# The last two output blocks by token halves, and the places of pass 3 moved into pass 1

## The chip, the cores and the metric

The kernel runs on one NeuronCore of one Trainium2 chip. The metric is the device time of one execution in microseconds (us), lower is better. The engines are named as in the profile: PE (TensorE matmul), PEld (its weight loads), DVE (VectorE), ACT (ScalarE), POOL (GpSimd) and SP, whose queue issues most transfers.

## The reference, cut to what matters

One decoder layer on 512 tokens of 1024 features, float32: token mixing (block-sparse attention and gated DeltaNet, merged), an output projection, and a mixture of experts. What the change touches begins at the output projection:

```python
x = x + g1 * (m @ w_out)                       # 8 output blocks of 128 features
h = rms_norm(x, norm2_w) * (1.0 + sc2) + sh2
pg = softmax(h @ w_rg + b_rg)                  # 4 groups: the best one
le = (h @ w_re + b_re).reshape(T, 4, 8)        # 8 experts in it: the best two
...
a = silu(h @ w_e_gate[e]) * (h @ w_e_up[e])    # for each chosen expert e
y += w2 * (a @ w_e_down[e])
x = x + g2 * y
out = rms_norm(x, final_norm_w)
```

## The kernel before

The program is traced in Python by a framework that orders each engine's instructions itself: an instruction that is traced earlier has priority, and one whose inputs are modelled as late may be passed by later ones. Two helpers pin the order. `tc.issue_after(x)` queues what is traced in it behind `x`, on `x`'s engine only. `Prog.step` does so for the last PE and the last SP instruction so far, so that all steps form one chain on PE and one on SP.

**`project_out`.** The features of `m` lie in SBUF as high and low parts. Output block `i` (128 features, all 512 tokens) is 8 x 3 matmuls (`mm3`, lines 138 to 140) of 128x512 into a PSUM tile `pj`; then DVE adds it to the residual `x1`, ACT squares it, and DVE adds the squares up in `asq`. The logits of blocks 0 to 5 are made in pairs, after blocks 1, 3 and 5 (line 1078), and the blocks 0 to 3 are turned to rows by `rows(i)` (four transposes, line 1050, and a copy on ACT). Block 7 alone is made in two halves of 256 tokens (`half`): `logits(h)` adds the half, makes its logits (1113) and sums of squares (1044), the inverse norm (`rsqrt`, 152 to 156), and then `choose(h)` (1218 to 1231) finds group and experts on DVE. A few matmuls on the identity (`warm`, line 214) are fillers. After the second half blocks 4 to 7 are turned to rows, and the rows are written to DRAM (`xd`).

**`moe`, up to pass 0.** `spread` (8 transposes), `route` (a filler, then `count`: for each token, how many before it chose the same expert, 10 small matmuls, and `pos0`), `sort` (counts per expert), `first_match` (line 1733: eight compares that make a one-hot matrix `ohf` from the places, and the split of the norms in three parts `MR`), `sorted`, a filler. The row gathers of pass 0 are matmuls of the rows with `ohf` (`first_rows`, line 1753), four feature blocks at a time.

**The passes.** Each of the 13 passes takes 128 places, in two to four experts: `up` (eight steps `block(k)`, line 1796, gate and up products), `gate`, `features` of the next pass (transposes, 1718, and copies on ACT and DVE), `add` of the pass before (1870 to 1872), `turn`, `down` (1847). For a pass from 3 on, `match(p)` (1645) compares on DVE, `places(p)` (1670, 1673) and `weights(p)` (1702, 1704) are small matmuls and reductions, and `fetch(p)` (POOL) gathers rows from `xd`. The expert weights come in units of 1 MB through a ring of 18 slots (line 1005, SP queue); 18 units are loaded ahead, and a slot is loaded again when its last product is done. Inside `up(0)`, `first_steps(k)` does ahead of block `k`: gathers, `places(1)`, `places(2)` (k = 0), the expert order (k = 2), `places(0)` (4) and `weights(0)` (7). Behind pass 0 stand `weights(1)`, `weights(2)`, `match(3)`, `places(3)` and `fetch(3)`, and only then `up(1)`.

Of the kernel before, what the change touches and what calls it, by code (L numbers as in the profile page):

```python
# [93 lines left out]
class Prog:  # L94
# [912 lines left out]
    def project_out(self):  # L1007
# [3 lines left out]
        with tc.tile_pool(name="ps_out", bufs=1, space=PSUM, reuse_waits="tile") as pp:  # L1011
# [40 lines left out]
            for i in range(7):  # L1052
                wh, wl = self.unit_w(None, self.wo[i])
                ps = pp.tile([128, 512], F32, name="pj", bufs=2)
                for k in range(8):
                    self.mm3(ps, wh[:, k], wl[:, k], self.mhi[:, k], self.mlo[:, k], k == 0, k == 7)
# [18 lines left out]
                if i in (1, 3, 5):  # L1075

                    for g in range(2):
                        mm(tiles(lt[64 * g:64 * g + 64]), w6[:, i - 1 + g], blk(i - 1 + g), start=i == 1, stop=i == 5)
                    if i == 5:
                        nc.scalar.activation(lT, tiles(lt), AF.Copy)  # L1080
                elif i == 6:
                    pr[0] = pp.tile([128, 512], F32, name="rt0")[:, 0:36]
                    for t in range(4):
                        mm(pr[t], lT[:, t], sel, start=True, stop=False)
                        mm(pr[t], x1[:, t], self.wr[:, 6], start=False, stop=False)
                if i in (1, 3):
                    rows(i - 1)
                    rows(i)
                if i == 3:
                    nc.scalar.dma_start(xv[:, :, 0:512], self.acc[:, :, 0:512])  # L1090
                if i == 6:
                    psq = pp.tile([128, 512], F32, name="tr", bufs=2)
                    for t in range(4):
                        sums(psq[:, t:t + 1], asq, t)
                    v.tensor_scalar(ss, psq[:, 0:4], 1.0 / D, EPS, op0=OP.mult, op1=OP.add)

            wh, wl = self.unit_w(None, self.wo[7])
            half = [pp.tile([128, 512], F32, name="pj", bufs=2) for _ in range(2)]
            x1 = blk(7)

            def products(h, ks):
                c = slice(256 * h, 256 * h + 256)
                for k in ks:
                    self.mm3(half[h][:, 0:256], wh[:, k], wl[:, k], self.mhi[:, k, c], self.mlo[:, k, c], k == 0, k == 7)

            def logits(h):
# [5 lines left out]
                for t in ts:  # L1112
                    mm(pr[t], x1[:, t], self.wr[:, 7], start=False, stop=True)
# [631 lines left out]
    def first_rows(self, *ks):  # L1745
# [3 lines left out]
        for k in ks:  # L1749
            ps[k] = self.bank()  # L1750
# [185 lines left out]
```

## Time and profile before

| | us |
|---|---|
| median of 3 runs | 724.14 (722.12 to 724.37) |
| the profiled execution | 724.38 |
| its span, first to last instruction | 722.5 |
| PE busy | 692.8 (96%) |
| DVE busy | 485.5 (67%) |
| ACT busy | 283.0 (39%) |
| moved by DMA | 183.12 MB, mean 253 GB/s |

Matmuls overlap one another, and their ends are modelled: the start of one to the start of the next is what one costs, and a busy PE is not PE at its peak. The idle time in brackets behind a row is that of its engine just before it, with what ended it. The granted clock is the share of full speed that TensorE was given in a stretch.

### The profile page before, as it was taken

Reading aid. Unit: us, or ns where it says so; the run is one execution under the profiler, and the core shown is the slowest. Engines: PE = TensorE matmul, PEld = TensorE weight load, DVE = VectorE, ACT = ScalarE, POOL = GpSimd, SP = SyncE. Lnnn points to the kernel's source line nnn. Section 1 sums busy time; section 2 is a strip of 40 time slices with the busy share of each in tenths; the row PEclk is TensorE's granted clock in tenths of the full one; section 3 lists DMA queues with packets and bytes.
Section 4 is the critical chain, followed back from the end, with each engine's and each line's share of the span. In section 5 each row is a group of like instructions: output and inputs, shape, how many; then the busy total and the mean of one; then the engine's idle time right before and its main releaser. Section 6 shows DMA issues by size and latency. Waiting matters only on the chain. (4 is left out here: it accounts for less than half of the span.)

```text
span 722.5 us, 10988 instructions
## 1 busy us (share of the span) xinstructions
PE 692.8 (96%) x3939; PEld 481.7 (67%) x3939; DVE 485.5 (67%) x1243; ACT 283.0 (39%) x554; POOL 36.1 (5%) x43
## 2 busy tenths in 40 slices
PE   7999999999999899999999999998899999999995
PEld 5887868878798777876778867793444444554531
DVE  6987669968447677578766744284577766777654
ACT  5745357652233224367652323143122222322352
POOL 0002000520000000000000000100000000000000
PEclk9999999999999999999999999999999999999998
DMA  9942221058765772361168998068799999999994
GB/s 357 394 168 69 97 85 62 30 149 295 215 235 191 250 251 89 120 232 60 44 215 282 340 422 354 2 237 322 277 351 418 418 415 404 419 417 418 427 418 190
DMA packets 47756, 183.12 MB, mean 253 GB/s; under 512 B 11786, under 2 KB 12330, under 8 KB 34514
## 3 DMA queue, kind: packets, MB, share of 16 engines
q1 hardware_dynamic: 40930, 169.65, 62.3%
q10 hardware_dynamic: 4896, 8.51, 3.3%
q0 software_dynamic: 1872, 4.23, 1.6%
q8 instruction: 32, 0.52, 0.3%
q14 instruction: 26, 0.21, 0.1%
HBM read 175.63 MB, written 9.33 MB: 256 GB/s over the span
## 5 line engine op out<-in xcount | busy, mean ns | idle before, releaser
L138 PE MATMUL pj<-hR,uR 128*128 128x512 f32 x304 | 122.3, 402 | 1.5 <-DVE qk L762 1.5
L140 PE MATMUL pj<-hR,uS 128*128 128x512 f32 x304 | 122.1, 402 | 0.0
L139 PE MATMUL pj<-hR,uR 128*128 128x512 f32 x304 | 122.0, 401 | 0.0
L143 ACT ACTIVATE uR<-uF 128x1024 fp32r<-128x1024 f32 x48 | 50.8, 1060 | 104.1 <-PE pj L139 97.3
L1796 PE MATMUL gu<-ra,uS 128*64 128x512 f32 (+1 forms) x368 | 85.0, 604 | 1.4 <-DMA ra<-w_e 1.4
L144 DVE TENSOR_TENSOR uS<-uF,uR 128x1024 fp32r<-128x1024 f32 x48 | 58.4, 1219 | 25.8 <-ACT uR L143 24.1
L138 PEld LDWEIGHTS pj<-hR,uR 128*128 128x128 f32 x304 | 57.3, 188 | 14.2 <-issue 1.9
L140 PEld LDWEIGHTS pj<-hR,uS 128*128 128x128 f32 x304 | 57.3, 188 | 12.5 <-DVE uS L144 0.4
L139 PEld LDWEIGHTS pj<-hR,uR 128*128 128x128 f32 x304 | 57.3, 188 | 11.9 <-issue 0.3
L1872 DVE TENSOR_TENSOR accF<-accF,cb 128x512 f32<-128x512 f32 x96 | 59.7, 680 | 6.3 <-PE cb L1871 5.4
L219 DVE SCALAR_TENSOR_TENSOR sgF<-sgF,misc 128x1024 f32<-128x1024 f32 x32 | 38.9, 1218 | 12.7 <-DMA sgF<-w_mod 12.7
L1796 PEld LDWEIGHTS gu<-ra,uS 128*64 128x64 f32 (+1 forms) x368 | 25.0, 125 | 32.5 <-issue 27.8
L1823 DVE SCALAR_TENSOR_TENSOR uS<-uS,meta,gu 128x256 f32<-128x256 f32 x13 | 6.2, 480 | 55.1 <-ACT uS L1818 55.1
L1860 ACT ACTIVATE uR<-p2F 128x512 fp32r<-128x512 f32 x24 | 15.1, 632 | 67.2 <-DVE p2F L1858 63.3
L1870 PE MATMUL cb<-uR,oht 128*128 128x512 f32 x96 | 40.0, 416 | 0.0
L1871 PE MATMUL cb<-uR,oht 128*128 128x512 f32 x96 | 37.9, 395 | 0.0
L1796 PE MATMUL gu<-rb,uS 128*32 128x512 f32 (+1 forms) x136 | 32.5, 593 | 0.0
L1818 ACT ACTIVATE uS<-gu 128x256 f32<-128x256 f32 x13 | 5.0, 384 | 64.9 <-PE gu L1796 64.9
L138 PE MATMUL pj<-mR,uR 128*128 128x512 f32 (+1 forms) x72 | 27.3, 379 | 0.0
L409 DVE SCALAR_TENSOR_TENSOR dF<-dF,c_cols 128x512 f32<-128x512 f32 x36 | 26.6, 748 | 0.9
L139 PE MATMUL pj<-mR,uR 128*128 128x512 f32 (+1 forms) x72 | 27.0, 375 | 0.0
L140 PE MATMUL pj<-mR,uS 128*128 128x512 f32 (+1 forms) x72 | 26.8, 372 | 0.0
(437 smaller groups left out, 1346.0 us busy)
## 6 DMA issues: line engine op xcount, KB each, us to landing
ra<-w_e SPq DMA_DIRECT2D x54, 1024.0 KB, 10.6
rb<-w_e SPq DMA_DIRECT2D x25, 1024.0 KB, 10.7
uF<-w_in SPq DMA_DIRECT2D x38, 512.0 KB, 3.3
sgF<-w_mod SPq DMA_DIRECT2D x32, 512.0 KB, 4.8
rc<-w_e SPq DMA_DIRECT2D x15, 1024.0 KB, 8.1
sF<-w_mod SPq DMA_DIRECT2D x8, 1024.0 KB, 9.0
gd<-sgF ACTq DMA_DIRECT2D x16, 256.0 KB, 2.8
gF<-gd SPq DMA_DIRECT2D x8, 512.0 KB, 4.5
```

The costliest lines, as they stand in the source:

```text
L138: mm(ps, whi, xhi, start=first, stop=False)
L139: mm(ps, whi, xlo, start=False, stop=False)
L140: mm(ps, wlo, xhi, start=False, stop=last)
L143: self.nc.scalar.activation(hi, raw, AF.Copy)
L144: self.nc.vector.tensor_sub(lo, raw, hi.bitcast(F32))
L219: self.nc.vector.scalar_tensor_tensor(raw, raw, 1.0, self.cact, op0=OP.mult, op1=OP.mult, accum_out=self.mod[:, ot:ot + 1])
L409: nc.vector.scalar_tensor_tensor(a, r[:, k:k + 512], w[:, k:k + 1], a, op0=OP.mult, op1=OP.add)
L1796: nc.tensor.matmul(gu[r], xe[:, k, r], w[:, k % 4], start=k == 0, stop=k == 7)
L1860: i1 = nc.scalar.activation(self.yhi[:, c], self.yf[:, c], AF.Copy)
L1870: nc.tensor.matmul(pc, self.oht[:, ts], self.yhi[:, c], start=True, stop=False)
L1871: nc.tensor.matmul(pc, self.oht[:, ts], self.ylo[:, c], start=False, stop=True)
L1872: nc.vector.tensor_add(self.acc[:, t, c], self.acc[:, t, c], pc)
```

## The change

Blocks 6 and 7 are both made by halves of the tokens: first half of block 6, sums of what came before, first half of block 7, second half of block 6, `logits(0)`, second half of block 7, `logits(1)`. Each half has its own sums of squares over both blocks. The pairs of logits are put inside the products of the next block (ahead of k = 2, or k = 4 of block 6). `count`, `first_match` and the first four gathers of pass 0 are split into tokens 0 to 255 and 256 to 511, and the first half's are traced ahead of the second half's count. `weights(0)` and `scale(1)`, `features(1, 0)` move into `up(0)`; `weights(1)`, `weights(2)`, `match(3)`, `places(3)`, `fetch(3)` and `match(4)` into `up(1)`. The fillers keep their sizes.

```diff
                 for t in range(4):
...
                 nc.scalar.activation(blk(i), p, AF.Copy)
-            for i in range(7):
+            def pair(i):
+                w = next(x for x in reversed(nc.cur_bb.bb.instructions) if x.engine == mybir.EngineType.PE)
+                for g in range(2):
+                    with tc.issue_after(w):
+                        w = mm(tiles(lt[64 * g:64 * g + 64]), w6[:, i + g], blk(i + g), start=i == 0, stop=i == 4).ins
+                if i == 4:
+                    nc.scalar.activation(lT, tiles(lt), AF.Copy)
+                else:
+                    with tc.issue_after(w):
+                        rows(i)
+                        rows(i + 1)
+                    if i == 2:
+                        nc.scalar.dma_start(xv[:, :, 0:512], self.acc[:, :, 0:512])
+                return w
+            for i in range(6):
                 wh, wl = self.unit_w(None, self.wo[i])
...
                 for k in range(8):
-                    self.mm3(ps, wh[:, k], wl[:, k], self.mhi[:, k], self.mlo[:, k], k == 0, k == 7)
+                    with ExitStack() as es:
+                        if k == 2 and i in (2, 4):
+                            es.enter_context(tc.issue_after(pair(i - 2)))
+                        self.mm3(ps, wh[:, k], wl[:, k], self.mhi[:, k], self.mlo[:, k], k == 0, k == 7)
                 x1 = blk(i)
...
                 if i == 0:
...
                         self.load(12)
...
                     self.load(1)
-                if i in (1, 3, 5):
...
+            ws = [self.unit_w(None, self.wo[i]) for i in (6, 7)]
+            two = [pp.tile([128, 512], F32, name="pj", bufs=2) for _ in range(2)]
+            def products(j, h):
                 c = slice(256 * h, 256 * h + 256)
-                for k in ks:
-                    self.mm3(half[h][:, 0:256], wh[:, k], wl[:, k], self.mhi[:, k, c], self.mlo[:, k, c], k == 0, k == 7)
+                wh, wl = ws[j]
+                for k in range(8):
+                    with ExitStack() as es:
+                        if (k, j, h) == (4, 0, 0):
+                            es.enter_context(tc.issue_after(pair(4)))
+                        self.mm3(two[j][:, c], wh[:, k], wl[:, k], self.mhi[:, k, c], self.mlo[:, k, c], k == 0, k == 7)
+            def added(j, h):
+                x1 = blk(6 + j)[:, 2 * h:2 * h + 2]
+                v.scalar_tensor_tensor(x1, tiles(two[j])[:, 2 * h:2 * h + 2], self.mod[:, 22 + j:23 + j], x1,
+                                       op0=OP.mult, op1=OP.add)
+                nc.scalar.activation(sq[:, 2 * j:2 * j + 2], x1, AF.Square)
+            def sums_before():
+                pr[0] = pp.tile([128, 512], F32, name="rt0")[:, 0:36]
+                for t in range(4):
+                    mm(pr[t], lT[:, t], sel, start=True, stop=False)
+                psq = pp.tile([128, 512], F32, name="tr", bufs=2)
+                for t in range(4):
+                    sums(psq[:, t:t + 1], asq, t)
+                v.tensor_scalar(ss, psq[:, 0:4], 1.0 / D, EPS, op0=OP.mult, op1=OP.add)
             def logits(h):
                 c, ts = slice(2 * h, 2 * h + 2), (2 * h, 2 * h + 1)
-                v.scalar_tensor_tensor(x1[:, c], half[h][:, 0:256].rearrange("p (t s) -> p t s", t=2), self.mod[:, 23:24],
-                                       x1[:, c], op0=OP.mult, op1=OP.add)
-                nc.scalar.activation(sq[:, c], x1[:, c], AF.Square)
                 psq = pp.tile([128, 512], F32, name="tr", bufs=2)
+                for j in range(2):
+                    for t in ts:
+                        mm(pr[t], blk(6 + j)[:, t], self.wr[:, 6 + j], start=False, stop=j == 1)
                 for t in ts:
-                    mm(pr[t], x1[:, t], self.wr[:, 7], start=False, stop=True)
-                for t in ts:
-                    sums(psq[:, t:t + 1], sq, t)
+                    for j in range(2):
+                        mm(psq[:, t:t + 1], sq[:, 2 * j + t % 2], self.ones[:, 0:1], start=j == 0, stop=j == 1)
                 v.scalar_tensor_tensor(ss[:, c], psq[:, c], 1.0 / D, ss[:, c], op0=OP.mult, op1=OP.add)
...
                 return w
-            products(0, range(8))
-            products(1, range(SPL))
+            products(0, 0)
+            added(0, 0)
+            sums_before()
+            products(1, 0)
+            added(1, 0)
+            products(0, 1)
             logits(0)
-            products(1, range(SPL, 8))
+            added(0, 1)
+            products(1, 1)
+            added(1, 1)
             w = logits(1)
...
                 for i in range(4, 8):
...
         selb = self.selb
...
         self.step(self.warm, self.gu.tile([128, 512], F32, name="gu"), self.ident, W2)
-        self.step(self.count, self.pos0)
-    def count(self, pos):
+    def count(self, pos, ts=range(4)):
         nc, v, selb, sel = self.nc, self.nc.vector, self.selb, self.sel
...
         ps = self.tr.tile([128, 512], F32, name="tr")
-        for t in range(4):
+        for t in ts:
             r = ps[:, 32 * t:32 * t + 32]
...
             nc.tensor.matmul(r, self.sut, selb[:, t], start=t == 0, stop=True)
-        v.tensor_scalar(sel, selb, -4096.0, 4096.0, op0=OP.mult, op1=OP.add)
-        v.tensor_tensor(fl(pos), fl(sel), ps[:, 0:128], op=OP.add)
+        c = slice(ts[0], ts[-1] + 1)
+        v.tensor_scalar(sel[:, c], selb[:, c], -4096.0, 4096.0, op0=OP.mult, op1=OP.add)
+        v.tensor_tensor(fl(pos[:, c]), fl(sel[:, c]), ps[:, 32 * ts[0]:32 * ts[-1] + 32], op=OP.add)
     def sort(self):
...
         self.last, self.after_down, self.fin = {}, (), {}
...
         self.step(self.route)
+        self.ohf, self.oh0 = V(self.uS, 4, [4, 128]), self.scratch(4, 64).bitcast(BF16)
+        self.rows_of = {k: self.bank() for k in range(4)}
+        self.step(self.count, self.pos0, (0, 1))
+        self.first_match((0, 1))
+        self.step(self.gather_first, (0, 1), range(4))
+        self.step(self.count, self.pos0, (2, 3))
         self.step(self.sort)
-        self.first_match()
+        self.first_match((2, 3))
+        self.first_parts()
         self.sorted()
...
         for x in self.xg:
...
                     for x in self.after_down:
...
                     self.scale(p + 1)
-            if 0 < p < NP - 3:
+            if 1 < p < NP - 3:
                 self.match(p + 3)
...
                 self.step(self.finish_init)
...
                     for x in self.after_down:
...
                     self.step(self.alike, p)
-            self.up(p, between=self.first_steps if p == 0 else None)
...
+            self.up(p, between=self.first_steps if p == 0 else self.second_steps if p == 1 else None)
             self.gate(p)
             if p + 1 < NP:
-                self.step(self.features, p + 1, 0)
-                if p == 0:
-                    self.step(self.features, 1, 1)
+                self.step(self.features, p + 1, int(p == 0))
             else:
...
             if p:
...
                     self.step(self.finish_last, h)
...
             self.step(self.load, len(PASSES[p]) - (p == 0))
-            if p == 0:
...
         self.last = {}
         self.rest()
...
                 nc.vector.tensor_scalar(xe[:, k], pt[:, j], self.A2[:, k:k + 1], self.sh2[:, k:k + 1],
                                         op0=OP.mult, op1=OP.add)
-    def first_match(self):
-        self.ohf, self.oh0 = self.view(self.uS, 4, [4, 128]), self.scratch(4, 64).bitcast(BF16)
-        for t in range(4):
+    def first_match(self, ts):
+        for t in ts:
             for e in range(2):
...
                                                  op0=OP.is_equal, op1=OP.mult)
+        self.at_match = i.ins
+    def first_parts(self):
         r, v = self.T(4), self.nc.vector
-        with self.tc.issue_after(i.ins):
+        with self.tc.issue_after(self.at_match):
             v.tensor_copy(r, self.rs2)
...
                     v.tensor_tensor(r, r, self.MR[:, :, j], op=OP.subtract)
-        self.at_match = i.ins
     def first_rows(self, *ks):
-        nc = self.nc
-        ps = {}
+        nc, ps = self.nc, self.rows_of
         for k in ks:
-            ps[k] = self.bank()
...
+            if k not in ps:
+                ps[k] = self.bank()
+        self.gather_first((2, 3) if ks[0] == 0 else range(4), ks)
         for k in ks:
...
                                  scale=self.A2[:, k:k + 1])
+    def gather_first(self, ts, ks):
+        for t in ts:
+            for k in ks:
+                self.nc.tensor.matmul(self.rows_of[k][:, 0:128], self.acc[:, t, 128 * k:128 * k + 128], self.ohf[:, t],
+                                      start=t == 0, stop=t == 3)
     def first_steps(self, k):
...
         elif k == 4:
...
             self.step(self.places, 0)
-        elif k == 7:
             self.step(self.weights, 0)
+        elif k == 6:
+            with self.tc.issue_after(self.at_tables):
+                self.scale(1)
+            self.step(self.features, 1, 0)
+    def second_steps(self, k):
+        if k == 3:
+            for i in (1, 2):
+                self.step(self.weights, i)
+            self.match(3)
+        elif k == 5:
+            self.step(self.places, 3)
+            self.fetch(3)
+            self.match(4)
     def up(self, p, experts=None, part=None, between=None):
```

## Rows read from the trace of the kernel before

**Rows 1.** The page's part 2: share of the 16 DMA engines in tenths and the bytes per second, in 40 equal slices of 18.06 us.

```profile
DMA  9942221058765772361168998068799999999994
GB/s 357 394 168 69 97 85 62 30 149 295 215 235 191 250 251 89 120 232 60 44 215 282 340 422 354 2 237 322 277 351 418 418 415 404 419 417 418 427 418 190
```

**Rows 2.** The view of busy time by stretch: us of the stretch, its length, then the busy us of PE, PEld, DVE, ACT and POOL (instructions in brackets), the granted TensorE clock, the mean share of the DMA engines and GB/s. The stretches are the last output blocks, the routing up to the first expert product, the gap behind pass 0, the first products of pass 1, and most of the passes behind.

```profile
455.00:472.00 17.00, 17.00 (x108) 14.10 (x109) 5.53 (x13) 3.19 (x6) 0.95 (x1) 1.00 0.00 1
472.00:489.20 17.20, 16.26 (x170) 15.56 (x168) 15.26 (x93) 9.18 (x20) 1.22 (x1) 1.00 0.78 270
...
503.70:507.70 4.00, 0.78 (x26) 0.69 (x24) 3.81 (x11) 1.87 (x3) 0.00 (x0) 1.00 1.00 363
507.70:516.40 8.70, 8.70 (x37) 2.63 (x33) 1.78 (x8) 0.00 (x0) 0.99 (x1) 0.80 0.55 171
...
532.00:688.00 156.00, 155.29 (x1053) 74.46 (x1049) 107.80 (x241) 42.40 (x92) 7.91 (x8) 1.00 1.01 416
```

**Rows 3.** The timeline of the SP queue, which issues the expert weights' loads, each as soon as its slot is free (start, us, queue, line, count).

```profile
493.40 0.93 SPq L1005 DMA_DIRECT2D ra<-w_e  x2
...
503.82 0.33 SPq L1005 DMA_DIRECT2D ra<-w_e  x1
...
513.12 1.50 SPq L1005 DMA_DIRECT2D ra<-w_e  x2
```

**Rows 4.** The timeline at the end, PE's weight load of the last pass's last products, with what ended the idle time ahead of it in brackets.

```profile
708.56 0.27 PEld L1847 LDWEIGHTS cb<-ra,uS 128*32 128x32 f32 x5 [0.16 <-DMA ra<-w_e]
```

**Rows 5.** PE's timeline from the end of pass 0 to the first products' end of pass 1, and for comparison the first products of pass 3 from their start (542.72) to the next instruction behind them (549.73).

```profile
503.68 0.35 PE L1702 MATMUL tr<-p2F,uS 128*128 128x6 bf16 x8
507.25 0.35 PE L1670 MATMUL tr<-MC,uS 128*128 128x1 bf16 x8 [3.22 <-DVE uS L1645]
507.74 5.35 PE L1796 MATMUL gu<-ra,uS 128*64 128x512 f32 x16
...
516.46 0.65 PE L1718 MATMUL tr<-ct,uF 128*128 128x128 f32 x4
...
542.72 0.63 PE L1796 MATMUL gu<-rc,uS 128*32 128x512 f32 x3
...
549.73 0.66 PE L1718 MATMUL tr<-ct,uF 128*128 128x128 f32 x4
```

**Rows 6.** DVE's timeline in the gap behind pass 0.

```profile
505.92 0.51 DVE L1704 TENSOR_REDUCE meta<-tr 64x1 f32<-64x3 f32 x3
506.44 0.76 DVE L1645 TENSOR_TENSOR uS<-ct,p2F 128x384 bf16<-128x384 f32 x2
...
508.63 0.88 DVE L1645 TENSOR_TENSOR uS<-ct,p2F 128x128 bf16<-128x128 f32 x2
```

**Rows 7.** Busy time by stretches of 2 us behind the gap, columns as in rows 2.

```profile
506.00:508.00 2.00, 0.74 (x18) 0.66 (x20) 1.96 (x7) 0.00 (x0) 0.00 (x0) 1.00 0.90 295
508.00:510.00 2.00, 2.00 (x8) 0.52 (x6) 1.48 (x8) 0.00 (x0) 0.57 (x1) 0.54 0.34 139
510.00:512.00 2.00, 2.00 (x8) 0.61 (x6) 0.00 (x0) 0.00 (x0) 0.42 (x1) 0.61 0.49 113
```

**Rows 8.** ACT's timeline between the first products and the down products of pass 0, and PE's first down product.

```profile
498.26 1.51 ACT L1722 ACTIVATE uS<-tr,mod,A 128x128 f32<-128x128 f32 x4 [0.23 <-PE tr L1718]
499.65 0.40 ACT L1832 ACTIVATE uS<-gu 128x256 f32<-128x256 f32 x1
...
500.10 0.64 PE L1847 MATMUL cb<-uR,uS 128*64 128x512 f32 x1 [1.06 <-ACT uS L1832]
```

**Rows 9.** PE's timeline in the output blocks: two products of 512 columns (block 6), then two of 256 (block 7).

```profile
462.31 0.40 PE L139 MATMUL pj<-mR,uR 128*128 128x512 f32 x1
462.55 0.39 PE L140 MATMUL pj<-mR,uS 128*128 128x512 f32 x1
...
471.79 0.28 PE L139 MATMUL pj<-mR,uR 128*128 128x256 f32 x1
471.90 0.28 PE L140 MATMUL pj<-mR,uS 128*128 128x256 f32 x1
```

**Rows 10.** PE's timeline from the last output product to the first expert product: fillers (L214), sums, transposes (L1050, L1536), counts (L1249), row gathers (L1753), places (L1670).

```profile
472.02 1.05 PE L214 MATMUL pj<-ct 128*128 128x128 f32 x8
...
473.31 0.59 PE L1044 MATMUL tr<-ct,oF 128*128 128x1 f32 x4
...
477.00 1.50 PE L214 MATMUL gu<-ct 128*128 128x128 f32 x12
479.05 0.18 PE L1249 MATMUL tr<-selb,sut 128*128 128x32 bf16 x1 [0.55 <-ACT p2F L1537]
...
480.67 3.74 PE L1753 MATMUL cb<-uS,accF 128*128 128x128 f32 x32
484.24 0.34 PE L1670 MATMUL tr<-MC,uS 128*128 128x1 bf16 x8
...
489.22 0.65 PE L1796 MATMUL gu<-ra,uS 128*64 128x512 f32 x2
```

**Rows 11.** The same time on ACT (the two banks of `spread` are copied out) and DVE (the eight compares of `first_match`, and the last of the parts that `places` reads).

```profile
478.42 1.06 ACT L1537 ACTIVATE p2F<-tr 128x512 f32<-128x512 f32 x2
...
479.96 1.87 DVE L1733 TENSOR_SCALAR uS<-ct,p2F,rs 128x64 f32<-128x64 f32 x8
...
483.83 0.15 DVE L1740 CAST p2F<-p2F 128x4 bf16<-128x4 f32 x1
```

More of the change, by code (lines that the diff above doesn't have):

```diff
@@ L1074, in project_out @@
                     self.load(1)
-                if i in (1, 3, 5):
[L1077 to L1082, printed above, removed]
-                    for t in range(4):
-                        mm(pr[t], lT[:, t], sel, start=True, stop=False)
-                        mm(pr[t], x1[:, t], self.wr[:, 6], start=False, stop=False)
@@ L1086, in project_out @@
[L1086 to L1092, printed above, removed]
-                    for t in range(4):
-                        sums(psq[:, t:t + 1], asq, t)
-                    v.tensor_scalar(ss, psq[:, 0:4], 1.0 / D, EPS, op0=OP.mult, op1=OP.add)
-            wh, wl = self.unit_w(None, self.wo[7])
@@ L1244, in count @@
         ps = self.tr.tile([128, 512], F32, name="tr")
-        for t in range(4):
+        for t in ts:
             r = ps[:, 32 * t:32 * t + 32]
@@ L1404, in moe @@
                     self.step(self.alike, p)
-            self.up(p, between=self.first_steps if p == 0 else None)
-            if p == 0:
-                with tc.issue_after(self.at_tables):
-                    self.scale(1)
+            self.up(p, between=self.first_steps if p == 0 else self.second_steps if p == 1 else None)
             self.gate(p)
             if p + 1 < NP:
-                self.step(self.features, p + 1, 0)
-                if p == 0:
-                    self.step(self.features, 1, 1)
+                self.step(self.features, p + 1, int(p == 0))
             else:
@@ L1448, in moe @@
             self.step(self.load, len(PASSES[p]) - (p == 0))
-            if p == 0:
-                for i in (1, 2):
-                    self.step(self.weights, i)
-                self.match(3)
-                self.step(self.places, 3)
-                self.fetch(3)
         self.last = {}
@@ L1742, in first_match @@
                     v.tensor_tensor(r, r, self.MR[:, :, j], op=OP.subtract)
-        self.at_match = i.ins
     def first_rows(self, *ks):
-        nc = self.nc
-        ps = {}
+        nc, ps = self.nc, self.rows_of
         for k in ks:
-            ps[k] = self.bank()
-        for t in range(4):
-            for k in ks:
-                nc.tensor.matmul(ps[k][:, 0:128], self.acc[:, t, 128 * k:128 * k + 128], self.ohf[:, t],
-                                 start=t == 0, stop=t == 3)
+            if k not in ps:
+                ps[k] = self.bank()
+        self.gather_first((2, 3) if ks[0] == 0 else range(4), ks)
         for k in ks:
```

4 lines of the change are left out of this document (removed).

## Prediction

> **What bounds the kernel now.** I read the page's slices first. The DMA engines stand still around 455 to 472 us and then, from the first expert pass on, run at over 400 GB/s to the end [rows 1]. Next the busy time by stretch: from 532 to 688 us PE is busy 155.29 of 156.00 us and the DMA share is 1.01, so both are full and neither can be squeezed there [rows 2]. The reader is to see the two places where one of them is not: from 472.0 to 489.2 us the DMA share is 0.78, and from 507.7 to 516.4 us it is 0.55, which is 3.9 us of idle DMA.
>
> The idle comes from the SP queue. A weight load is issued when PE has freed its slot, at 493.40, at 503.82 and then only at 513.12 us [rows 3]. So ahead of 532 us PE sets when the loads go out, and behind it all that is left is a fixed amount of loads and products that slides with them. At the end the last weight loads of the last pass are still waited for, by 0.16 us, at 708.56 us [rows 4]: PE and the loads arrive together. A microsecond that PE wins ahead of 516 us is therefore a microsecond of the end, as long as there is idle DMA time to move the loads into. That makes the sum a sum of PE's time from 455 to 516 us.
>
> **The change, part 1: later places moved.** Pass 0 ends with PE's `weights` at 503.68 us. Then PE waits 3.22 us, for the compare of `match(3)` on DVE, before `places(3)` at 507.25 us and the first products of pass 1 at 507.74 us [rows 5]. That compare came last because DVE first had the reductions (to 506.43 us) and then took 0.76 us [rows 6]. The wait has a second cost: the granted clock was 1.00 up to 508 us, and after the wait 0.54 and 0.61 in the two stretches from 508 to 512 us [rows 7], so part of that time ran at the lower of the two levels, 1.2 GHz in place of 2.4. The first products of pass 1 took 516.46 - 507.74 = 8.72 us, those of pass 3 only 549.73 - 542.72 = 7.01 us [rows 5]: 1.71 us more.
>
> With the change `weights(1)` and `weights(2)` stand ahead of block 3 of pass 1's first products and `places(3)` ahead of block 5, so the first products can follow pass 0 at once; their input was written during pass 0. From 503.68 to 516.46 us is 12.78 us now. It becomes 7.01 us of products, 0.35 us for the two `weights` and 507.74 - 507.25 = 0.49 us for `places(3)` [rows 5], together 7.85 us. **The gain is 4.9 us.** What must hide: `match(3)` now has to run on DVE between block 3 and block 5. Two blocks are 2 x 7.01/8 = 1.75 us; the reductions and the compare took about 0.65 and 0.76 us, 1.41 us together [rows 6], so the margin is some 0.3 us less what signals cost. If that fails, PE stops inside pass 1 instead. `match(4)` (some 1.4 us of DVE) moves behind it and is needed only after the first products end. `fetch(3)` is issued on POOL with nothing queued behind it; its 0.5 MB takes 1.3 us at the 416 GB/s of the full stretch and falls into the stretch with 3.9 us idle [rows 2].
>
> `features(1, 0)` moves into pass 0's products ahead of block 6: four transposes, about 0.5 us more for PE there. In return ACT's four copies (1.51 us from 498.26) no longer stand ahead of the copy at 499.65 us for which the down products waited 1.06 us [rows 8]; about 0.5 us comes back. I take 0, with -0.5 and +0.5 as bounds. `weights(0)` and `scale(1)` move with no wait to gain or lose that I can see.
>
> **Part 2: blocks 6 and 7 by halves, pairs moved.** Two successive products of 512 columns start 0.24 us apart, of 256 columns 0.11 us apart (462.31 and 462.55; 471.79 and 471.90) [rows 9], so 24 products of block 6 become 48 in the same time. PE is busy 17.00 of 17.00 us from 455 to 472 us [rows 2], with the pairs of logits in it: moving them elsewhere cannot win time, and what they wait for (a block's sum on DVE) is older when they run later. I take 0, and 0.3 us each way. The Trainium skill's page "TensorE: Matmul & The Clock Gate", section "Back-to-back issue gap", gives N/2.4 + 2.5 ns for the gap of a matmul, so it speaks against splitting: 24 more matmuls would add 0.06 us, where the rows show no extra, and the sum stays what it is by either.
>
> The sums of squares and the logits of block 7 were 16 PE instructions for both halves and those of block 6 eight; squares of block 6 were added on DVE. Now both blocks have their own sums: 8 PE instructions more, all in the second half's part behind the last product. At 3.57/32 = 0.112 us each (the 32 gather instructions from 480.67 to 484.24 us) that is +0.9 us [rows 10].
>
> **Part 3: the first half's experts, places and gathers.** The text of the change wants these under the second half. But the calls are chained on PE: `spread`, the filler of `route`, then `count` for the first half, its gathers, `count` for the second half, `sort`, the filler, and the rest. None can pass the other, and all stand behind the transposes. From 472.0 to 489.2 us PE is busy 16.26 of 17.20 us [rows 2]: 0.94 us can be won at the very most, and the added 0.9 us eats it. So 0 is the floor of this part.
>
> Now the path. The count at 479.05 us waited 0.55 us for ACT's copy of `spread` [rows 10]; ACT's copies [rows 11] come after the transposes, so all moves by 0.9 us to 479.95 us. From count to the first gather: compares began 0.91 us after the count's start (479.96) and take 1.87/8 = 0.234 us each [rows 11]; two are needed, so 1.38 us, with nothing in PE's queue that may pass. The first half's 16 gathers run 481.33 to 483.12 us. Only then comes the second half's count; to its gathers it is 1.62 us as before (479.05 to 480.67, filled by counts and filler) [rows 10], so 484.74 to 486.53 us, where the gathers ended at 484.24 us. On DVE the second half's four compares end at 483.12 + 0.91 + 0.94 = 484.97 us, and the parts that `places(1)` reads were ready 2.15 us behind the last compare (483.98 after 481.83) [rows 11]: 487.12 us. `places(1)` began at 484.24 us and needs them 0.2 us in, so this is **2.7 us late at worst**. Fillers and transposes behind the last product are not in the chain, and may be put into the two holes of 0.55 and 1.38 us; then it is 2.7 - 1.9 = 0.8 us. Between 0.8 and 2.7 I take **+1.9 us**, nearer the upper end because in the rows of before the transposes follow the sums directly and the fillers stand ahead of them.
>
> **Sum.** -4.9 + 1.9 = -3.0 us. The profiled execution took 724.38 us (span 722.5), so 721.4 us by its own time; it lies 0.24 us above the median of 724.14, so 721.1 us for the median.
>
> **The rivals.** (a) *The halves pay.* The scheduler fills both holes and the second half's shorter work on DVE is felt: part 3 costs 0, its floor. 724.14 - 4.9 = 719.2 us. For it: the first half's choice is ready long ahead. Against it: PE's queue is nearly full. (b) *The clock falls ahead of pass 0.* The new holes stand among transposes and tiny counts. If the clock falls there as it did behind the 3.22 us wait, the price is that row's 1.7 us: 722.8 us. Against it: 0.55 us holes among the same work left it at 1.00 [rows 2]. The Trainium skill's page "TensorE: Matmul & The Clock Gate", section "Part 4: PE-mode transpose", says that transposes do not count as PE-busy for the clock; by that rule this rival would be likelier, but the trace holds 24 transposes in a row at 1.00. (c) *The loads don't follow.* If only the idle DMA time of 507.7 to 516.4 us can be won, less the 1.3 us of `fetch(3)` that now falls among the loads, the gain is 2.6 in place of 4.9 us: 723.4 us. Against it: the whole train of loads moves, not only those. (d) *Slower: the wait moves along.* `match(3)` on DVE may not begin before `weights(1)` has read the buffer that it overwrites, at block 3. If DVE puts `scale(2)` and `match(4)` ahead of it, PE stops at block 5 for as long as it did before and the clock falls with it; the 4.9 us are gone and part 3's worst case stays: 724.14 + 2.7 = 726.8 us. It decides from a wait of about 1.4 us (what `match(4)` lasts) on; below that the sum holds its sign.
>
> **How the numbers follow.** The sum 47 in 100 (its own range 719.8 to 722.4), (a) 20, (b) 13, (c) 10, (d) 10. Some 0.3% (2.2 us) is what a measurement of this kernel can tell from no change, so faster is below 722.0: four fifths of the sum's case and all of (a), 0.59; (b), (c) and the rest of the sum are within, 0.31; (d) is slower, 0.10. The range goes from (a) with the 0.5 and 0.3 us bounds of parts 1 and 2, 718.4, up past (b) and (c) with 1.5 us for part 3's upper end, 724.9; only (d) is left out.
>
> **What would show it.** Right: no wait of PE between pass 0's down products and pass 1's first products, these in some 7.8 us at a clock of 1.00, load issues 9.3 us apart (503.82 to 513.12) now some 4.9 us closer; the first expert product about 1.9 us later than 489.22 us, with a hole between the first half's count and its gathers. Wrong: the first expert product earlier than 489 us, a wait ahead of block 5, or a lower clock between 480 and 490 us.

## The result and the profile after

The changed kernel took 716.88 us, median of 4 runs (716.47 to 720.52), where the kernel before took 724.14. The ratio of the runs is 0.9921 (95% interval 0.9892 to 0.995), and with the changed kernel run again beside the experiments 0.9916 (0.9884 to 0.9948): about 6 us faster. The forecast was 721.1 with a range from 718.4; the ratio puts the kernel at the range's edge (0.9921 x 724.14 = 718.4), the median 1.5 us below it. The direction was right, the gain about twice the forecast. The range reached so low only for rival (a), the halves that pay, and that is not what happened; that the time lies at this edge is luck.

The profiled execution of the changed kernel is the slowest of its four, 720.52 us (span 718.7). Its work ahead of the output projection, which the change doesn't touch, ended 2.84 us later than before. So I compare stages, from a fixed point on: the small product with the biases (L1027, at 420.91 in place of 418.07 us), which runs inside the first output block, behind 16 of its 24 products, in every kernel. The expectations below call it the first output product. Each number is the difference between the starts of two instructions in PE's timeline, in us: A from that point to the last output product; B on to the first expert product; C to the first product of pass 1; D to the first instruction behind pass 1's first products (a transpose, L1718 before and L1734 after); E to the end of the span, which is known to 0.1 us.

| kernel | start | A | B | C | D | E | ratio to before (95%) |
|---|---|---|---|---|---|---|---|
| before | 418.07 | 53.83 | 17.32 | 18.52 | 8.72 | 206.04 | |
| after | 420.91 | 50.26 | 19.80 | 14.28 | 8.05 | 205.40 | 0.9921 (0.9892 to 0.995) |
| after, again (e10) | 418.42 | 50.26 | 19.80 | 14.28 | 8.04 | 205.40 | 0.9916 (0.9884 to 0.9948) |
| e1 pairs | 418.07 | 50.19 | 17.32 | 18.52 | 7.02 | 206.38 | 0.9944 (0.9918 to 0.9969) |
| e2 places | 421.58 | 53.86 | 17.32 | 14.39 | 8.04 | 205.61 | 0.9923 (0.9894 to 0.9951) |
| e3 whole | 416.71 | 50.27 | 17.80 | 14.66 | 8.04 | 205.52 | 0.9903 (0.9874 to 0.9933) |
| e4 apart | 416.71 | 54.51 | 19.80 | 14.28 | 8.05 | 206.35 | 0.9987 (0.9961 to 1.0012) |
| e5 both | 416.10 | 50.20 | 17.32 | 14.42 | 8.04 | 205.52 | 0.9871 (0.983 to 0.9911) |
| e6 early | 419.41 | 50.26 | 18.19 | 14.28 | 8.04 | 205.42 | 0.988 (0.9836 to 0.9924) |
| e7 fill | 417.59 | 53.85 | 17.33 | 18.52 | 7.02 | 205.89 | 0.9973 (0.9944 to 1.0001) |
| e8 late | 418.30 | 50.26 | 19.80 | 14.28 | 9.40 | 205.56 | 0.994 (0.9911 to 0.997) |
| e9 half | 420.87 | 50.93 | 19.79 | 14.58 | 8.05 | 205.38 | 0.9909 (0.9878 to 0.9939) |
| e11 both, again | 424.45 | 50.19 | 17.31 | 14.29 | 8.04 | 205.72 | 0.9854 (0.9825 to 0.9883) |
| before, again (e12) | 418.22 | 53.85 | 17.32 | 18.55 | 9.63 | 206.33 | one run |

From before to after the stages change by -3.57 (A), +2.48 (B), -4.24 (C), -0.67 (D) and -0.64 us (E), together -6.64. The forecast had 0, +1.9, and -4.9 for C and D together. A to C repeat within 0.4 us wherever the code of the stage is the same; the start doesn't (416.10 to 424.45). The small differences are therefore read from the stages, the ratios only confirm.

**Stage A, where 0 was forecast.** PE's timeline around the first pair of logits, first of the kernel before, then after; a product of a pair is two instructions.

```profile
425.95 1.07 PE L1078 MATMUL rt<-accF,oF 128*64 128x512 f32 x2
426.96 0.50 PE L138 MATMUL pj<-mR,uR 128*128 128x512 f32 x1
427.39 1.07 PE L1078 MATMUL rt<-accF,oF 128*64 128x512 f32 x2
428.39 0.66 PE L1050 MATMUL tr<-ct,accF 128*128 128x128 f32 x4
```

```profile
429.86 0.40 PE L140 MATMUL pj<-mR,uS 128*128 128x512 f32 x1
430.19 1.08 PE L1057 MATMUL rt<-accF,oF 128*64 128x512 f32 x4
431.20 0.66 PE L1050 MATMUL tr<-ct,accF 128*128 128x128 f32 x4
```

The reader is to see `128*64`: each product of a pair uses 64 of the array's 128 columns. Before, one full product stood between the two, and the three took 428.39 - 425.95 = 2.44 us. After, all four instructions of a pair take 1.01 us, what one product alone took before: the two run beside each other. PE is busy in both cases.

**Stage B, where +1.9 was forecast.** PE's timeline, to be laid beside [rows 10].

```profile
471.17 0.28 PE L140 MATMUL pj<-mR,uS 128*128 128x256 f32 x1
...
478.80 0.18 PE L1268 MATMUL tr<-selb,sut 128*128 128x32 bf16 x1 [0.55 <-ACT p2F L1553]
...
479.91 2.05 PE L1776 MATMUL cb<-uS,accF 128*128 128x128 f32 x16 [0.89 <-DVE uS L1748]
481.80 0.20 PE L1267 MATMUL tr<-selb,one 128*128 128x32 bf16 x2
...
483.14 2.05 PE L1776 MATMUL cb<-uS,accF 128*128 128x128 f32 x16
485.03 0.34 PE L1686 MATMUL tr<-MC,uS 128*128 128x1 bf16 x8
486.20 0.24 PE L1689 MATMUL tr<-p2F,uS 128*128 128x3 bf16 x4 [0.83 <-DVE p2F L1758]
...
490.97 0.65 PE L1830 MATMUL gu<-ra,uS 128*64 128x512 f32 x2
```

Both holes of the prediction are there: 0.55 us ahead of the first half's count and 0.89 ahead of its gathers. The places, of which it said that they would come late, wait 0.83 us for the second half's parts.

**Stages C and D, where -4.9 was forecast.** PE's timeline behind pass 0, beside [rows 5].

```profile
505.25 2.74 PE L1830 MATMUL gu<-ra,uS 128*64 128x512 f32 x12
507.93 0.35 PE L1718 MATMUL tr<-p2F,uS 128*128 128x6 bf16 x8
...
510.08 0.35 PE L1686 MATMUL tr<-MC,uS 128*128 128x1 bf16 x8
...
513.30 0.66 PE L1734 MATMUL tr<-ct,uF 128*128 128x128 f32 x4
```

There is no bracket: neither the weights at block 3 nor the places at block 5 wait. From the end of pass 0 to 513.30 us it is 8.05 us, where it was 12.78 [rows 5]. The clock by 2 us, in the columns of [rows 7]:

```profile
508.00:510.00 2.00, 2.00 (x16) 0.68 (x16) 1.73 (x7) 0.00 (x0) 0.00 (x0) 1.00 0.85 332
510.00:512.00 2.00, 2.00 (x26) 1.04 (x26) 1.55 (x8) 0.00 (x0) 0.00 (x0) 1.00 0.87 270
```

Full clock, and DMA shares of 0.85 and 0.87 where they were 0.34 and 0.49 [rows 7]. The SP queue, beside [rows 3]:

```profile
505.49 4.16 SPq L1005 DMA_DIRECT2D ra<-w_e  x2
...
509.32 1.49 SPq L1005 DMA_DIRECT2D ra<-w_e  x2
```

The load that had to wait until 513.12 us is now the one at 509.32 us (the second of the first line, the first of the other): 3.83 us behind the load ahead of it, where it was 9.30 [rows 3]. The loads followed PE, and E is no longer than before.

### The profile page after: what moved, and what is told of

Read it like the earlier page. It is cut to its first block, busy times and chain, and to the rows that moved or that the text cites. A ratio compares the mean times of both kernels' runs of the same rounds, so it can differ in the third digit from the quotient of the medians.

```text
span 718.7 us, 11057 instructions
## 1 busy us (share of the span) xinstructions
PE 692.3 (96%) x3971; PEld 486.2 (68%) x3971; DVE 486.7 (68%) x1245; ACT 283.2 (39%) x555; POOL 36.4 (5%) x43
## 5 line engine op out<-in xcount | busy, mean ns | idle before, releaser
L1830 PE MATMUL gu<-ra,uS 128*64 128x512 f32 (+1 forms) x368 | 83.5, 594 | 0.5 <-DMA ra<-w_e 0.5
L138 PE MATMUL pj<-mR,uR 128*128 128x512 f32 (+1 forms) x80 | 28.4, 355 | 0.0
L139 PE MATMUL pj<-mR,uR 128*128 128x512 f32 (+1 forms) x80 | 28.2, 353 | 0.0
```

Source lines behind the costliest of these rows:

```text
L138: mm(ps, whi, xhi, start=first, stop=False)
L139: mm(ps, whi, xlo, start=False, stop=False)
L1830: nc.tensor.matmul(gu[r], xe[:, k, r], w[:, k % 4], start=k == 0, stop=k == 7)
```

## The experiments

Each line number is that of the kernel run. The theory: the pairs win in A because their products run beside each other; the moved places win in C and D; the halves' counts and gathers cost in B. The rivals are in the expectations.

**e1, e2: each part alone.** e1 is the kernel before with pairs of neighbours, e2 the kernel before with the later places moved (the hunks of the diff for `second_steps`, `first_steps` and the loop over passes).

```
+            def pair(i):
+                w = next(x for x in reversed(nc.cur_bb.bb.instructions) if x.engine == mybir.EngineType.PE)
+                for g in range(2):
+                    with tc.issue_after(w):
+                        w = mm(tiles(lt[64 * g:64 * g + 64]), w6[:, i + g], blk(i + g), start=i == 0, stop=i == 4).ins
...
+                        if k == 2 and i in (2, 4, 6):
+                            es.enter_context(tc.issue_after(pair(i - 2)))
```

> The kernel before, with one part of the change alone: the two products of a pair of logits issued directly behind each other (in blocks 2, 4 and 6, behind the second of eight steps), blocks 6 and 7 whole, places where they were. Theory A (the two products of a pair fill 64 columns of the array each and run beside each other when nothing stands between them): each pair takes 1.0 us in place of 2.0 and something, 1.2 us a pair, so 3.6 us off the output projection and off the end, about 720.5. Rival B (the prediction's term: a pair only moves, PE is full in either case): 0, 724.1. Rival C (the 3.6 us seen come from the halves of blocks 6 and 7): 0 as well, and the four products of a pair still take 2.0 us.

> The kernel before, with the other part alone: the later places, weights, features and scale moved into the products of passes 0 and 1, the output projection as it was. The prediction's sum: 12.78 us behind pass 0 become 7.85 to 8.05, 4.7 to 4.9 us, all of which reaches the end, 719.3. Rival (the loads don't follow, rival c of the prediction): 2.6 us, 721.5. Rival (the places move a wait into block 5, rival d): 0, 724.1.

e1: A is 50.19, 3.64 us less than before, with blocks 6 and 7 as they were, so the pairs alone give it. B and C didn't move. e2: C fell by 4.13 and D by 0.68 to 8.04, 4.8 us together, and E by 0.43; the part alone gives what was forecast, and none of it is lost behind.

**e1 and e12: the clock behind the wait.** e1 held a surprise. It still has the wait of 3.22 us behind pass 0, but D is 7.02. Its timeline of PE and its busy time by stretch:

```profile
503.61 0.35 PE L1677 MATMUL tr<-MC,uS 128*128 128x1 bf16 x8 [3.22 <-DVE uS L1652]
```

```profile
504.00:511.00 7.00, 7.00 (x39) 2.28 (x35) 1.83 (x8) 0.00 (x0) 0.99 (x1) 1.00 0.53 170
```

The same wait, and the clock stayed at 1.00. So the kernel before was run once more.

> The kernel before itself, one more execution, for the clock behind the wait of 3.22 us alone. Theory A (the fall of the clock there belongs to the execution: the same wait was followed by 1.00 in the run with the pairs moved): pass 1's first products may take 7.0 us at 1.00, and if they do, A is shown. Theory B (it belongs to this program, and moving the pairs ended it): 8.7 us and 0.5 to 0.6 in every execution; a second 8.7 us would leave both standing.

```profile
507.43 0.37 PE L1670 MATMUL tr<-MC,uS 128*128 128x1 bf16 x8 [3.22 <-DVE uS L1645]
```

```profile
506.00:508.00 2.00, 0.57 (x18) 0.56 (x18) 1.95 (x8) 0.00 (x0) 0.00 (x0) 0.60 0.97 369
508.00:510.00 2.00, 2.00 (x7) 0.71 (x8) 1.65 (x8) 0.00 (x0) 0.40 (x1) 0.50 0.33 131
510.00:512.00 2.00, 2.00 (x6) 0.47 (x4) 0.00 (x0) 0.00 (x0) 0.59 (x1) 0.50 0.37 74
```

It fell again, earlier, and D took 9.63 us. Theory A is not shown by it, since no execution of this very program kept its clock. But B's 8.7 us in every execution is not what came either: one program, one wait of 3.22 us, and the price was 1.70 us in one execution and 2.61 in the other (over 7.02). That moving the pairs has something to do with e1's full clock is therefore not excluded.

**e7: the wait filled.** Thirteen fillers in PE's order between `weights(2)` and `match(3)` of the kernel before.

```
                 for i in (1, 2):
                     self.step(self.weights, i)
+                self.step(self.warm, self.gu.tile([128, 512], F32, name="gu"), self.ident, 13)
                 self.match(3)
```

> The kernel before with 13 fillers (products of the identity, 128 columns) in PE's order inside the wait of 3.22 us behind pass 0. Theory (the clock falls because PE stands still there): the granted clock stays at 1.00 from 508 to 512 us, pass 1's first products take 7.0 us in place of 8.72, and the kernel is 1.7 us faster or a little less, as far as the fillers outlast the wait. Rival (the clock falls for another reason, the small products at the end of pass 0 or the load on the engine): 0.6 again in that stretch, no gain or up to 1 us slower.

```profile
503.45 3.15 PE L214 MATMUL gu<-ct 128*128 128x128 f32 x26
506.80 0.35 PE L1671 MATMUL tr<-MC,uS 128*128 128x1 bf16 x8 [0.21 <-DVE uS L1646]
```

The clock was 1.00 throughout, C stayed at 18.52 and D was 7.02: 1.70 us won, as the theory has it. Since e1 had the same 7.02 us without fillers, one execution doesn't prove that the fillers did it, and the ratio's interval reaches 1. Inconclusive by itself.

**e4, e9: what parts a pair.** A filler between the two products of each pair of the changed kernel; in e4 over the full width of the array, in e9 over the 64 columns in which the second product runs.

```
                 for g in range(2):
+                    if g:
+                        with tc.issue_after(w):
+                            w = self.warm(pp.tile([128, 512], F32, name="pj", bufs=2), self.ident, 1).ins
```

```
+                    if g:
+                        z = pp.tile([128, 512], F32, name="pj", bufs=2)
+                        with tc.issue_after(w):
+                            w = mm(z[64:128, 0:128], self.ident[:, 0:64], self.ident, start=True, stop=True).ins
```

> The changed kernel with one filler (a product of the identity, 128 columns over the full width of the array, two instructions) between the two products of each pair; nothing else is moved. Theory A (the two run beside each other only if nothing of full width stands between them): some 1.0 us and the filler's 0.1 to 0.2 for each of three pairs, 3.3 to 3.9 us slower than the changed kernel. Rival (standing together is no matter; what was won is the place that they moved to): only the fillers, 0.3 to 0.6 us.

> The changed kernel with a filler between the two products of each pair, as in the earlier run with fillers, but of 64 columns, the same half of the array in which the second product of the pair runs. Theory (what parts the pair is a product over the full width, which has to wait for both halves; a product in the other half runs beside the first): each pair takes 1.0 us and at most 0.2 more for the filler, and the kernel is 0.2 to 0.6 us slower than the changed one. Rival (any instruction between the two parts them, because the halves run beside each other only if their products are neighbours): 2.0 us and more a pair, 3.0 to 4.2 us slower, as with the filler of full width.

PE's timeline of e4 and then of e9:

```profile
425.99 1.07 PE L1060 MATMUL rt<-accF,oF 128*64 128x512 f32 x2
426.99 0.49 PE L214 MATMUL pj<-ct 128*128 128x128 f32 x2
427.41 1.07 PE L1060 MATMUL rt<-accF,oF 128*64 128x512 f32 x2
428.41 1.09 PE L1050 MATMUL tr<-ct,accF 128*128 128x128 f32 x8
```

```profile
430.15 0.64 PE L1061 MATMUL rt<-accF,oF 128*64 128x512 f32 x1
430.16 0.43 PE L1059 MATMUL pj<-ct 128*64 128x128 f32 x2
430.43 1.02 PE L1061 MATMUL rt<-accF,oF 128*64 128x512 f32 x3
431.38 0.66 PE L1050 MATMUL tr<-ct,accF 128*128 128x128 f32 x4
```

With the filler of full width a pair takes 2.42 us and A is 4.25 us longer: the whole gain of the pairs is gone, and the ratio is 0.9987. That is more than the 3.3 to 3.9 us of the forecast, because the filler itself takes 0.42 us (426.99 to 427.41) and not 0.1 to 0.2. With the filler in one half a pair takes 1.23 us and A is 0.67 us longer, just above the forecast's 0.6 (the ratio, 0.9909, doesn't tell it from the changed kernel); the filler starts 0.01 us behind the first product. So it is not the place they moved to, and not that they are neighbours, but that nothing of full width stands between them.

**e3, e6: what the halves cost.** e3 is the changed kernel with the counts, first compares and first gathers whole again; e6 issues the first half's count and compares ahead of `spread`.

```
...
-        self.step(self.count, self.pos0, (0, 1))
-        self.first_match((0, 1))
-        self.step(self.gather_first, (0, 1), range(4))
-        self.step(self.count, self.pos0, (2, 3))
...
+        self.step(self.count, self.pos0)
         self.step(self.sort)
-        self.first_match((2, 3))
+        self.first_match(range(4))
...
-        self.gather_first((2, 3) if ks[0] == 0 else range(4), ks)
+        self.gather_first(range(4), ks)
```

```
+        self.step(self.count, self.pos0, (0, 1))
+        self.first_match((0, 1))
         self.step(self.spread, self.g2r, self.mod[:, 40:48])
         self.step(self.route)
...
-        self.step(self.count, self.pos0, (0, 1))
-        self.first_match((0, 1))
         self.step(self.gather_first, (0, 1), range(4))
```

> The changed kernel with the count, the first compares and the first gathers for both halves at once again, as before the change; blocks 6 and 7 stay in halves with their own sums. Theory (a chain of PE's order: the first half's gathers wait for its compares, and the second half's count stands behind them): the first expert product comes 1.6 to 2.5 us earlier behind the last output product, and the kernel is as much faster than the changed one, 0.3% of it. Rival (the halves pay for themselves, and the longer way to the first expert product comes from the 8 more PE instructions and the later sums of squares alone): 0, or up to 1 us slower.

> The changed kernel with the first half's count and compares issued ahead of the spread and its filler, its gathers behind them, so that the compares run under eight products and six fillers of PE. Theory (the chain of PE's order between the first half's count and its gathers is what the halves cost): the wait of 0.9 us ahead of the gathers goes, and the one of 0.5 us ahead of the first count with it; the first expert product comes 1.0 to 1.8 us earlier behind the last output product (18.0 to 18.8 us in place of 19.8). Rival (the second half's chain sets it, whatever the first does): 19.8 us still, no change.

e3: B is 17.80, so 2.00 of the 2.48 us come from the order of counts and gathers, inside the forecast's 1.6 to 2.5. The other 0.48 stay with the halves' own sums, transposes and squares, which e3 keeps; they were not taken apart. Its C is 0.38 longer; C is 14.58 in e9 too, which changes nothing there, so I leave that out. The ratios of e3 and of the changed kernel (0.9903 and 0.9921) have intervals that overlap, so only the stage shows it. e6: PE's timeline shows where the waits went.

```profile
475.66 0.65 PE L1552 MATMUL tr<-ct,mod 128*128 128x128 f32 x4 [0.58 <-DVE p2F L1270]
...
477.49 1.95 PE L1776 MATMUL cb<-uS,accF 128*128 128x128 f32 x16
...
483.08 0.24 PE L1689 MATMUL tr<-p2F,uS 128*128 128x3 bf16 x4 [0.36 <-DVE p2F L1758]
```

The gathers no longer wait, and B is 1.61 us shorter, inside the forecast's 1.0 to 1.8. A wait of 0.58 us has taken the place of the 0.55 ahead of the count (the spread's own transposes now wait for DVE), and the one ahead of the places shrank from 0.83 to 0.36. It is still 0.87 us longer than B with no halves.

**e8: the cover taken away.** In the changed kernel `weights(1)`, `weights(2)` and `match(3)` go from block 3 to block 5, directly ahead of `places(3)`.

```
-        if k == 3:
+        if k == 5:
             for i in (1, 2):
                 self.step(self.weights, i)
             self.match(3)
-        elif k == 5:
             self.step(self.places, 3)
```

> The changed kernel with the compares of the fourth places (and the two weights ahead of them) issued at block 5 of pass 1's first products, directly ahead of the places that read them, in place of block 3. Theory (the two blocks between are what hides them): PE waits 1.0 to 1.6 us at block 5 for DVE's compare, and the kernel is as much slower. Rival (DVE is free early enough in any case): no wait over 0.3 us, 0.

```profile
508.83 0.35 PE L1686 MATMUL tr<-MC,uS 128*128 128x1 bf16 x8 [1.44 <-DVE uS L1661]
```

The wait is there, D is 9.40 (+1.35), the clock stayed at 1.00 (by stretches of 2 us from 500 to 514 us), so the two blocks are the cover. The ratio (0.994 where the changed kernel has 0.992) is too coarse to show 1.35 us by itself.

**e5, e11, e10: both gains without the halves.** The edits of e1 and e2 in one kernel; run twice, the second time beside the changed kernel.

> The kernel before with the pairs moved and the later places moved, and without the halves: block 7 alone in halves as before, its sums as before, counts, first compares and first gathers whole. Theory (the two parts add, the halves only cost): 50.2 us from the first to the last output product, 17.3 us from there to the first expert product, 14.4 us from there to pass 1's first products; with 3.6 and 4.7 us won, 716.2 where the kernel before takes 724.5, 2.5 us less than the changed kernel. Rival (what the pairs win is waited for again, because loads then arrive last): not more than 5 us won, 719.5.

> The kernel before with the pairs and the later places moved and without the halves, once more, beside the changed kernel on the same chip. Theory (the halves only cost): 2.5 us less than the changed kernel, 8.3 less than the kernel before, a ratio of 0.9885. Rival (its earlier lead was the chip's): level with the changed kernel.

> The changed kernel itself, unchanged, for a ratio from as many runs as the experiments have. By the stages of its profile (3.6 and 4.7 us won, 2.5 lost) 5.8 us less than the kernel before, a ratio of 0.992.

The stages add as the theory has it: 50.20, 17.32, 14.42. The medians are 715.91 and 714.92 us; beside the latter the changed kernel has 718.56, and the intervals, 0.9825 to 0.9883 and 0.9884 to 0.9948, just don't meet. The expected lead was 2.5 us, the medians give 3.6. It beats both kernels.

## Why the prediction was right and wrong

**What bounds it: right.** What PE won ahead of pass 1 arrived at the end: E is 205.38 to 206.38 us in every kernel, whatever was won ahead of it. Rival (c), that the loads don't follow, is out: with the places alone moved (e2) C and D are 4.8 us shorter and E is no longer.

**Part 1: right, one term worth less certainty.** C and D fell by 4.91 us where 4.9 was worked out, but two small errors meet in that. From the end of pass 0 on, where the sum was made, it is 12.78 - 8.05 = 4.73 us, since products, weights and places took 8.05 us in place of 7.85; the other 0.18 came inside pass 0 (14.46 us from its first product before, 14.28 after), where the prediction took 0, with 0.5 either way. The wait's 3.22 us are sure. The 1.71 us for the clock were read from one execution and taken as fixed; the same wait cost 0 (e1), 1.70 and 2.61 us (e12). So this part is worth 3.2 us (18.52 + 7.02 against 14.28 + 8.05) to 5.9 (18.55 + 9.63), if the 7.02 of e1 can come in the kernel before too, which no execution here showed. Rival (d) didn't come: `match(3)` was ready in time, and e8 shows that its price would have been 1.35 us, the clock not falling behind a wait of 1.44 us.

**Part 2: wrong, and this is the step that failed:** "moving them elsewhere cannot win time". I took PE's 17.00 of 17.00 us busy [rows 2] for a full array. A product of 64 columns leaves half of it free, and a busy PE doesn't show that; the shapes in the timeline do. The trace of before held a sign of it: at 500.10 us two down products of 64 columns start together, one of which stands in [rows 8]. The part gave 3.57 us in A, and e1, e4 and e9 show by what. The Trainium skill's page "TensorE: Matmul & The Clock Gate", section "Part 3: Packing small matmuls — row/col tiling", says that products in separate parts of the array run at the same time. The trace agrees: two products that alone take 1.0 us each take 1.01 together. The section also says that products start and end in the order in which they were issued. The trace of e9 doesn't agree: both instructions of the filler start (the first at 430.16 us) ahead of the second instruction of the product that stands before it in PE's order (430.43 at the earliest). That fits an order kept in each half by itself, which a full product in between would join again (2.42 us in e4); it was not tested further. The halves of blocks 6 and 7 cost 0.07 us in A (50.26 against 50.19 in e1 and e11), though the pairs stand at other places in them and this was not taken apart. The prediction's estimate from the Trainium skill's page "TensorE: Matmul & The Clock Gate", section "Back-to-back issue gap", was 0.06 us.

**Part 3: right in sign and mechanism, 0.6 us short.** +2.48 against +1.9 taken and 2.7 as the worst. The chain (count, hole, gathers, count) cost 2.00 of them (e3). The other 0.48, where 0.9 us of more instructions was forecast, stays with the halves' own work, which e3 keeps and e5 hasn't. The part taken off for fillers in the holes was wrong: none went into the holes of 0.55, 0.89 and 0.83 us. Rival (a), that the halves pay, is out: B is 17.3 us wherever there are none.

**Rival (b), the clock ahead of pass 0,** didn't come: between 455 and 505 us no stretch of 2 us in any of these kernels fell below 1.00, with transposes, counts and waits of 0.9 us in it. The rule on transposes that was weighed for it (the Trainium skill, "TensorE: Matmul & The Clock Gate", section "Part 4: PE-mode transpose") is not tested by this: 24 transposes in a row (473.76 to 477.00 us before) brought no fall, but products of other kinds stand on both sides of them.

**Sum.** Forecast -4.9 + 0 + 1.9 = -3.0. Measured -4.9 - 3.6 + 2.5 = -6.0 us, and -0.6 in E. E is 205.4 to 205.7 us in all kernels with the places moved but one (e4, 206.35) and 205.9 to 206.4 in those without; why, and why e4 is apart, stays open.

## What to carry to other kernels

Busy time of PE says that it is occupied, not that its array is full: read the shapes, and where two products use 64 columns each in different halves, issue them with nothing of full width between them. Splitting a stage to start half of it early can cost more than it gives: here each half brought its own wait (2.48 us), and with the first half's compares covered by other products of PE it still cost 0.87 (e6). A price for the clock that was read behind one wait in one execution is a draw, not a constant: put the wait in the sum, and the clock's part in the range.

## What the runs showed of the hardware that was not expected

- Two products of 64 columns and 512 elements took 1.01 us together beside each other and 2.42 to 2.44 us with a full product between them; a small product in one of the halves added 0.22 us (e9).
- The step from a full product to one of 64 columns takes longer than from full to full: 429.86 to 430.19 us is 0.33 us, where two successive full products start 0.24 us apart [rows 9]. The two kinds also differ in time per element (1.0 us against 0.24 for 512), so that the width is the cause is not shown.
- The clock behind the same 3.22 us wait was at the higher level in one execution (e1) and fell to the lower, 1.2 GHz, for part of the next microseconds in two others (0.54 and 0.61 [rows 7]; 0.60, 0.50 and 0.50 in e12). Between e11 and e5, two executions of one kernel, two longer waits and such falls behind them make the difference in the start of stage A. From 19 to 192 us their products keep 0.31 to 0.35 us apart. Then e11 waits 2.14 us for a DMA (e5 waits 0.20) and runs on at the lower level. PE's timeline of e11, and busy time by stretch of e11 and then of e5:

```profile
194.47 1.92 PE L604 MATMUL ax<-dF 128*128 128x64 f32 x12 [2.14 <-DMA dF<-dx]
```

```profile
190.00:210.00 20.00, 17.86 (x90) 15.09 (x89) 4.89 (x8) 3.83 (x8) 0.00 (x0) 0.83 0.48 134
```

```profile
190.00:210.00 20.00, 19.80 (x134) 17.54 (x132) 8.66 (x14) 6.56 (x13) 0.00 (x0) 1.00 0.63 180
```

By 204 us e11 is 5.4 us behind, 1.9 of it the longer wait. A wait of 2.27 us for DVE (249.59 us) with a second fall (0.72 from 250 to 256 us, 1.00 in e5) takes it to 8.8; it reaches stage A at 424.45 us, e5 at 416.10. So the clock fell behind waits of 2.14 and 2.27 us and not behind 3.22 us in e1 or 1.44 in e8. What decides it stays open here.

- A granted clock of 1.00 at the very start of a profile can be wrong. These are the first 20 us and a row of PE's timeline of e11, then of e5:

```profile
0.00:20.00 20.00, 13.63 (x61) 11.81 (x62) 13.35 (x48) 11.03 (x19) 0.20 (x4) 0.74 0.93 363
12.05 3.78 PE L290 MATMUL tr<-sF 128*128 128x128 f32 x16 [5.31 <-ACT sF L279]
```

```profile
0.00:20.00 20.00, 15.09 (x63) 11.79 (x63) 12.91 (x48) 10.46 (x19) 0.20 (x4) 1.00 0.93 363
12.70 3.79 PE L290 MATMUL tr<-sF 128*128 128x128 f32 x16 [3.85 <-ACT sF L279]
```

The clock is given as 0.50 from 12 to 16 us in e11 and as 1.00 in e5. Yet the 16 transposes take the same time in both, about 0.22 us each, where transposes of the same shape behind a pair start 0.11 us apart. So e5's ran at the lower level too, and the two executions leave this stretch 0.3 us apart. The clocks that the stages above rest on agree with the durations (7.02 us of D at 1.00).
